# Neighbourhood attention trunk: a run's loads in one sequence, headed by a wait for a third of the transposes

## The chip, the cores and the metric

One core of a Trainium2 chip runs the whole kernel as one program. The metric is device time in microseconds; three runs of the kernel before gave 991.87, 992.1 and 993.92, so its median is 992.1. The profile is of one execution, on the hardware, with every instruction recorded.

## The reference

One layer of an encoder over 2048 tokens of 1024 columns, in float32. The tokens are a grid of 32 rows by 64 columns.

```python
h = rmsnorm(x, g)
q, k, v, gate = split(h @ w_in, 4)              # w_in: 1024 x 4096; 16 heads of 64
s = q . k / 8 + rel_pos_bias                    # each token sees 8 rows x 16 columns of the grid
o = softmax(s) @ v
x = x + (o * silu(gate)) @ w_out                # w_out: 1024 x 1024
out = rmsnorm(x, norm_f)
```

## The kernel before

All matrices are split into a high and a low part, so that a product of two takes three matmuls; large products are made from seven half-size products instead of eight. The order of every engine's instructions is written out by the program itself, in Python; nothing is rescheduled afterwards.

The program has three parts. In the first (to about 560 us) `stage_one` and `stage_two` form most of the queries, keys, values and gates and store them in HBM (`qd`, `kd`, `vd`, `sgd`). The second is the attention, 32 *runs* (lists `order`, `cycles = 32`): a run is a pair of heads `p` with a quarter `T` of the tokens. The third (`rows_by_seven`, from about 870 us) forms the output product and the last normalisation.

The main loop (L1825) has one body for each run. Body m does, in this order:

- `begin(m)` (L1804) puts the loads of the body on a list of things that fall due;
- `feed(...)` gives TensorE *fill*: some 14 matmuls per run of the remaining projections (L384 to L388) or, later, of the output product (L1600 to L1604). Each matmul of the fill advances a counted clock by one, and `due` (L336) issues whatever on the list has come due by that clock. The clock is counted while the program is written; nothing of it is read on the chip;
- `turns(m-1)` (L1358): 48 transposes on TensorE (L1372, tiles `ph`) turn the probabilities of run m-1, in three thirds `b`; after each third ScalarE and VectorE copy the two `ph` banks to the tile `PT` (named `pta`; L1378, L1376). Behind them GpSimd clears parts of the probability tiles (L1308, `clear_x`);
- `scores(2m)` and `scores(2m+1)` (L1310): 64 matmuls `s` of queries and keys (L1323), then on VectorE the sum with the bias table (L1332) and on ScalarE the exponential (L1340);
- `values(m-1)` (L1382): 36 matmuls `o` of `pta` and the values (L1395), then the product with the gates (L1399) and, 4 counts later, the store to `ogd` (L1402).

What a run reads from HBM is loaded by SyncE, in order, one DMA after the other:

- queries, `load_q` (L1243, tile `q`, 256 KB, two buffers);
- keys, `load_k` (L1226, tile `kt`, 128 to 512 KB; one buffer for even and one for odd `p`, and a run of the same `p` adds to it);
- two bias tables, `load_bias` (L1268, tile `em`, 184 or 253 KB each, ten buffers);
- values, `load_v` (L1252, tile `vt`, 480 KB, two buffers);
- gates, `load_sg` (L1260, tile `sgt`, 256 KB, two buffers).

Before, `begin(m)` asks for the gates of run m-1, the tables, queries and keys of run m+1 and the values of run m, in this order, one every half count from 0.5 on. On the chip SyncE issues a DMA when the ones ahead of it are issued, when the tile's last reader is done, and when the DMA eight places before it has landed, because eight completion semaphores are used in turn. A load thus goes out as soon as its buffer is free: the queries wait for the last scores matmul of the run that had the buffer (L1248), the values for its last `o` matmul (L1258).

In the same queue stand the weights of the fill (`raw`, L161 and L163), the stores, and from the last runs on the weights and rows of the third part: `land_first` (L1628) loads nine weights `t` at 1.5 counts of the last run's body, and six loads of attention output (`raw<-ogd`, L1656) follow from 10 counts on.

Of the kernel before, what the change touches and what calls it, by code (L numbers as in the profile page):

```python
# [61 lines left out]
def build(ctx, tc, x, xr, xt, wg, bias, w_out, n0, nf, out):  # L62
    nc = tc.nc
# [56 lines left out]
    def bank(n, name):  # L120
        return banks.tile([128, n], F32, name=name, tag="bank")
# [208 lines left out]
    def store(key, lag, f):  # L330
        n = len(later)
        while n and later[n - 1][0] > clock[0] + lag:
            n -= 1
        later.insert(n, (clock[0] + lag, key, f))
# [8 lines left out]
    def must(*keys):  # L343
        assert all(k in written for k in keys), keys
        for n in range(len(later) - 1, -1, -1):
            if later[n][1] in keys:
                for _ in range(n + 1):
                    later.pop(0)[2]()
                break
# [869 lines left out]
    KT, VT, QT, EM, SG = {}, {}, {}, {}, {}  # L1219
    stored_at = {}  # L1220
    order = [(p, T) for p in range(NP) for T in (1, 0)] + [(p, T) for p in range(NP - 2) for T in (2, 3)]
# [4 lines left out]
    def load_k(p, T):  # L1226
        r0, r1, more = PARTS[T]
        base = 12 * (T > 1)
        a, b = r0 * GW, r1 * GW + more
        must(*[("k", p, c) for c in range(a // 512, (b + 511) // 512)])  # L1230

        def keys():
            if T in (1, 2):
                khalf.clear()
                KT[p, T // 2] = (kp([128, 2048], F32, "kt") if p % 2 == 0 else mkp([128, 1536], F32, "kt"))[:, :1344]
            t = KT[p, T // 2]
            if T == 2:
                nc.gpsimd.memset(t[:, 1280:1288], 0.0)
            nc.sync.dma_start(t[:, a - base * GW:b - base * GW], kd[p][:, a:b])

        return keys

    def load_q(p, T):  # L1243
        must(("q", p, T))

        def queries():
            QT[p, T] = qp([128, 512], F32, "q")
            nc.sync.dma_start(QT[p, T], qd[p][T])  # L1248

        return queries  # L1250

    def load_v(p, T):  # L1252
        r0, r1 = FRAME[T], FRAME[T] + TALL
        must(*[("v", p // 4, t) for t in range(r0 // 2, (r1 + 1) // 2)])
        rows = vd[p // 4][p % 4][r0 * 8192:r1 * 8192].rearrange("(k x) -> k x", x=1024)
        t = vp([128, 1024], F32, "vt")
        VT[p, T] = t.rearrange("p (s d) -> p s d", s=8)
        nc.sync.dma_start(t[:8 * TALL], rows)  # L1258

    def load_sg(p, T):  # L1260
        must(("g", p, T))
        SG[p, T] = sp([128, 512], F32, "sgt")
        nc.sync.dma_start(SG[p, T], sgd[p][T])
# [4 lines left out]
    def load_bias(p, T):  # L1268
        fs = []
        kind = BRINGS[T]  # L1270
        w = 2 * WIDE * TABLES[kind][2]
        EM[p, T // 2, kind] = []
        for quad in range(2):
            t = mp([128, 512], F32, "em")[:, :w]
            EM[p, T // 2, kind].append([t[:, :w // 2], t[:, w // 2:]])
            o = TABLE_AT[kind] + quad * w
            fs.append(lambda t=t, o=o, w=w: nc.sync.dma_start(t, bias[p, 128 * o:128 * (o + w)].rearrange("(q c) -> q c", c=w)))
        return fs

    X, PT, ST = {}, {}, {}  # L1280
# [18 lines left out]
    def clear_x(T):  # L1299
        stale = []  # L1300
        for half in range(2):
            (u0, n0), (u1, n1) = held[half], HALF_ROWS[T][half]
            held[half] = u1, n1
            stale += [(half, a, b - a) for a, b in ((u0, min(u0 + n0, u1)), (max(u0, u1 + n1), u0 + n0)) if a < b]
        for quad in range(2):
            for half, a, n in stale:
                for s in range(2):
                    nc.gpsimd.memset(by_strip(X[quad, half, s], (a, n)), 0.0)  # L1308
# [49 lines left out]
    def turns(m):  # L1358
        p, T = order[m]
        k = 8 * TALL  # L1360
        PT[m] = pt([128, 3072], F32, "pta")
        t = PT[m].rearrange("p (s b n c) -> p b s n c", s=2, b=3, c=64)
        for b in range(3):
            ph = [bank(512, f"ph{h}") for h in range(2)]
            at = (2 - b) * k
            for quad in range(2):
                for half in range(2):
                    for s in range(2):
                        for h in range(2):
                            q = slice(64 * h, 64 * h + 64)  # L1370
                            o = s * 256 + half * 128 + quad * 64
                            nc.tensor.transpose(ph[h][:k, o:o + 64], X[quad, half, s][q, at:at + k], ident[q, q])  # L1372
            for h in range(2):
                o, i_ = t[:k, b, :, h::2], ph[h][:k].rearrange("p (s n c) -> p s n c", s=2, c=64)
                if h:
                    nc.vector.tensor_copy(o, i_)  # L1376
                else:
                    nc.scalar.activation(o, i_, AF.Copy)  # L1378
        if m + 1 < cycles:
            clear_x(order[m + 1][1])  # L1380

# [170 lines left out]
    def rows_due():  # L1552
        n = ready["split"]
        return (n < ready["loaded"] and "turn" in ready and place[n] <= ready["turn"] + 3 and now() - late["loaded_at"][n] >= 40 \
                and sum(1 if hasattr(g, "rearrange") else 2 for g in G.values()) <= 6)
# [95 lines left out]
    def load_rows_of(m, f, home=None):  # L1651
        n, half = PAIRS[m][int(f[1]) - 1], int(f[2]) - 1
        T, i = divmod(n, 4)
        must(*[("og", p, T) for p in range(NP) if p // 4 == half])
        A[m, f] = (home or raw)([128, 512], F32, "raw")
        nc.sync.dma_start(A[m, f].rearrange("p (k q) -> p k q", k=4), ogd[T][i, half])  # L1656
# [108 lines left out]
    cycles = len(order)  # L1765
# [30 lines left out]
    def later_loads(fs, lag, step):  # L1796
        for k, f in enumerate(fs):
            store(("load",), lag + k * step, f)

    def all_loads():  # L1800
        while any(e[1][0] == "load" for e in later):
            later.pop(0)[2]()

    def begin(m):  # L1804
        all_loads()
        quiet[0] = False
        fs = [lambda: load_sg(*order[m - 1])] if m else []
        if m + 1 < cycles:
            nx = order[m + 1]
            fs += load_bias(*nx)  # L1810
            fs += [load_q(*nx), load_k(*nx)]
        if m < cycles:
            fs.append(lambda: load_v(*order[m]))
        later_loads(fs, 0.5, 0.5)
        if m == cycles - 1:
            later_loads([land_first], 1.5, 0)
            later_loads([lambda f=f, i=i: load_rows_of(i, f) for i in ((2, 0, 1) if PLAIN <= 6 else (0, 1)) for f in ("A11", "A12")], 10, 0.5)
        if m == cycles:
            later_loads([land_rest], 4, 0)
# [5 lines left out]
    for m in range(cycles + 1):  # L1825
        a = amount[m] - 8
        begin(m)
        feed(HALF_HEAD)
        if m:
            normalise(2 * m - 1, 0)  # L1830
        feed(HEAD - HALF_HEAD)
        if m:
# [5 lines left out]
            most, behind = 99 if a > 12 else 0 if rows_due() else 1, bool(rooted)  # L1838
# [19 lines left out]
        if m:  # L1858
            turns(m - 1)
# [58 lines left out]
```

## Time and profile before

| | |
|---|---|
| runs of the kernel, us | 991.87, 992.1, 993.92 |
| profiled execution, us | 993.25 |
| its span, us | 991.5 |
| instructions | 22624 |
| granted TensorE clock | 0.999 of full speed |
| HBM read and written | 160.37 MB and 66.06 MB |
| attention runs | about 574 to 871 us, some 9.3 us each |

How to read it: PE is TensorE's matmuls, PEld its weight loads, DVE VectorE, ACT ScalarE, POOL GpSimd, SP SyncE; "SPq" is a DMA issue in SyncE's queue. L and a number is the line of the program. `ph<-ident,x` is an instruction that writes tile `ph` and reads `ident` and `x`. In the table of waits stand, for an engine and a line, whom it waited for, the total in us, how often, and the longest. "issue" there and in the chain is time in which an engine waited for nothing that the profile shows. A row of a stretch table has the stretch, its length, and busy time and count for PE, PEld, DVE, ACT and POOL, then the granted clock, the DMA engines' mean share and GB/s. A row of the DMA list has the issue, its count, its size, and the median time from issue to landing. A row of a DMA queue has its packets, their MB and the share of the 16 DMA engines.

### The profile page before, as it was taken

What the parts mean: (1) busy time and instruction counts of PE and PEld (TensorE: products, weight loads), DVE (VectorE), ACT (ScalarE), POOL (GpSimd) and SP (SyncE); (2) the same over time, 40 slices, a digit from 0 to 9 for tenths busy, and PEclk for the clock granted to TensorE, in tenths of its full rate; (3) what the DMA queues carried; (4) which work ended last, traced back from release to release, by engine and by line L of the source; (5) the groups of instructions that cost most, each with busy time, mean ns of one, the idle gap of its engine ahead of it and who ended that gap; (6) DMA issues with size and microseconds to landing.
All of it is one profiled execution on the core that took longest, in us unless ns stands there. A gap on an engine that the chain in (4) does not pass through costs nothing.

```text
span 991.5 us, 22624 instructions
## 1 busy us (share of the span) xinstructions
PE 979.3 (99%) x8172; PEld 797.0 (80%) x8172; DVE 755.2 (76%) x1735; ACT 531.5 (54%) x1310; POOL 159.6 (16%) x430
## 2 busy tenths in 40 slices
PE   9999999999999999999999999999999999999997
PEld 7888888888888888888888778777778777888886
DVE  6899888988665876766775677668778878877866
ACT  7773245455535342343433467677777776654443
POOL 0000001231100000000001133333343332302110
PEclk9999999999999999999999999999999999999999
DMA  8943547777957836657565799878989978697754
GB/s 287 337 130 102 196 132 256 248 242 251 368 159 225 276 116 201 189 182 224 169 176 203 247 302 271 264 226 279 307 277 288 298 222 266 223 379 212 205 146 117
DMA packets 149968, 227.93 MB, mean 230 GB/s; under 512 B 13536, under 2 KB 66016, under 8 KB 149856
## 3 DMA queue, kind: packets, MB, share of 16 engines
q1 hardware_dynamic: 146832, 221.37, 70.2%
q0 software_dynamic: 2592, 4.72, 2.8%
q8 instruction: 64, 1.05, 0.4%
q14 instruction: 48, 0.39, 0.1%
q10 hardware_dynamic: 432, 0.40, 0.1%
HBM read 160.37 MB, written 66.06 MB: 228 GB/s over the span
## 4 chain that ended last, share of the span: by engine, by line
PE 99%; issue 1%; DVE 0%; ACT 0%
PE pp L446 40%; PE pv L612 13%; PE py L1695 12%; PE o L1395 8%; PE s L1323 6%; PE ph L1372 5%; PE pp L388 2%; PE pp L384 2%; PE pp L386 2%; PE pv L727 2%; PE po L1600 2%; PE po L1604 2%; PE po L1602 2%; PE zp L127 0%; PE prb L235 0%
## 5 line engine op out<-in xcount | busy, mean ns | idle before, releaser
L446 PE MATMUL pp<-h,f 128*128 128x512 f32 x576 | 185.3, 389 | 0.0
L446 PE MATMUL pp<-t,f 128*128 128x512 f32 x702 | 171.4, 389 | 0.0
L446 PEld LDWEIGHTS pp<-t,f 128*128 128x128 f32 x702 | 131.8, 188 | 27.4
L1340 ACT ACTIVATE x<-sums,st 128x264 f32<-128x264 f32 (+1 forms) x256 | 124.5, 488 | 30.0 <-DVE st L1332 30.0
L446 PEld LDWEIGHTS pp<-h,f 128*128 128x128 f32 x576 | 108.1, 188 | 22.6
L446 PE MATMUL pp<-l,f 128*128 128x512 f32 x288 | 112.0, 389 | 0.0
L1352 POOL TENSOR_SCALAR x<-x,st 128x264 f32<-128x264 f32 (+1 forms) x192 | 88.5, 477 | 113.7 <-DVE st L1347 93.8
L1332 DVE CUSTOM_DVE_ANT_0 sums<-s,em 128x253 f32<-128x253 f32 (+1 forms) x256 | 91.1, 401 | 6.2 <-ACT x L1340 1.7
L429 DVE TENSOR_TENSOR f<-raw,f 128x512 fp32r<-128x512 f32 x105 | 75.9, 727 | 19.4 <-ACT f L428 19.3
L1395 PE MATMUL o<-pta,vt 120*64 120x192 f32 (+2 forms) x1152 | 85.1, 300 | 4.0 <-issue 4.0
L1395 PEld LDWEIGHTS o<-pta,vt 120*64 120x64 f32 x1152 | 70.2, 137 | 23.2 <-issue 16.4
L428 ACT ACTIVATE f<-raw 128x512 fp32r<-128x512 f32 x105 | 63.4, 622 | 36.6 <-DVE raw L435 22.0
L1376 DVE COPY pta<-ph 120x512 f32<-120x512 f32 x96 | 60.3, 684 | 18.3 <-PE ph L1372 18.1
L1378 ACT ACTIVATE pta<-ph 120x512 f32<-120x512 f32 x96 | 50.4, 599 | 37.8 <-PE ph L1372 37.8
L446 PEld LDWEIGHTS pp<-l,f 128*128 128x128 f32 x288 | 54.0, 188 | 11.3
L1323 PE MATMUL s<-kt,q 64*32 64x253 f32 (+1 forms) x2048 | 59.2, 362 | 0.7 <-issue 0.7
L1372 PEld LDWEIGHTS ph<-ident,x 64*120 64x120 f32 x1536 | 47.6, 135 | 11.3 <-issue 10.6
L612 PE MATMUL pv<-wh,t 128*128 128x512 f32 x176 | 56.2, 389 | 0.0
L1695 PE MATMUL py<-woh,f 128*128 128x512 f32 x168 | 55.4, 390 | 0.0
L467 POOL TENSOR_TENSOR tmp<-tmp,rb 128x512 f32<-128x512 f32 x18 | 28.5, 1582 | 157.6 <-DVE tmp L464 137.2
L446 PE MATMUL pp<-sixths,f 128*128 128x512 f32 x198 | 52.7, 389 | 0.0
L1372 PE MATMUL ph<-ident,x 64*120 64x64 f32 x1536 | 52.0, 221 | 0.0
(231 smaller groups left out, 1889.4 us busy)
## 6 DMA issues: line engine op xcount, KB each, us to landing
raw<-in_wg_dram SPq DMA_DIRECT2D x124, 256.0 KB, 4.8
vt<-vd SPq DMA_DIRECT2D x32, 480.0 KB, 5.2
row<-in_xr_dram SPq DMA_DIRECT2D x32, 256.0 KB, 5.2
vd<-v SPq DMA_DIRECT2D x32, 256.0 KB, 3.2
sgd<-sg SPq DMA_DIRECT2D x32, 256.0 KB, 3.8
q<-qd SPq DMA_DIRECT2D x32, 256.0 KB, 3.6
sgt<-sgd SPq DMA_DIRECT2D x32, 256.0 KB, 5.3
ogd<-og SPq DMA_DIRECT2D x32, 256.0 KB, 5.3
```

Of the source, the lines that this page charges most:

```text
L428: nc.scalar.activation(t[:, 0], src, AF.Copy)
L429: nc.vector.tensor_tensor(t[:, 1], src, t[:, 0].bitcast(F32), OP.subtract)
L446: nc.tensor.matmul(B[n, P], t[:, int(m == 2), c], x[k][int(m == 1)], start=P in (1, 6, 5) and k == 0 and m == 0, stop=k == 3 and m == 2, s ...
L612: nc.tensor.matmul(p, a[:, o], b, start=P in (1, 6, 5) and k == 0 and m == 0, stop=k == 3 and m == 2, skip_group_check=True)
L1323: nc.tensor.matmul(places[half, s][h * 32:h * 32 + 32], qt[a, g * 64 + half * 32:g * 64 + half * 32 + 32], kt[a, o:o + n * GW].rearrange(" ...
L1332: nc.vector.tensor_tensor_reduce(rows[s][:, :, :WIDE], places[half, s].rearrange("p (r c) -> p r c", c=WIDE), table[s].rearrange("p (r c) ...
L1340: nc.scalar.activation(to, rows[s].rearrange("p r (b c) -> p b r c", b=3), AF.Exp, bias=st[:, o:o + 1], scale=-1.0, accum_out=st[:, 4 + o: ...
L1352: nc.gpsimd.tensor_scalar(t, t, f, 1.0, op0=OP.mult, op1=OP.mult)
L1372: nc.tensor.transpose(ph[h][:k, o:o + 64], X[quad, half, s][q, at:at + k], ident[q, q])
L1376: nc.vector.tensor_copy(o, i_)
L1395: nc.tensor.matmul(o[s * 64:s * 64 + 64, g0 * 64:g1 * 64], vt[:k, strip, s * 64:s * 64 + 64], moving, start=strip == 0, stop=strip == 7, s ...
L1695: nc.tensor.matmul(B[m, P], t[:, a, c], b, start=P in (1, 6, 5) and k == 0 and i == 0, stop=k == 3 and i == 2, skip_group_check=True)
```

## The change

`load_q` takes an argument. Where it is given a part of a tile, GpSimd first copies its eight elements into the new query tile, and the DMA of the queries, which overwrites the tile, therefore waits for that copy. The new function `loads_of(m)` issues without any lag the queries, keys and tables of run m+1, then the values and gates of run m (the last run's gates excepted). It is called once in `begin(0)` for run 0, and from then on inside `turns(m)`, after the first third (`b == 0`), for run m+1, with the first eight elements of `PT[m]`, which ScalarE's first copy of that third has written. `begin` keeps the last run's gates, and the loads of the third part. Nothing that is computed changes.

```diff
     def load_q(p, T):
         must(("q", p, T))
 
-        def queries():
+        def queries(behind=None):
             QT[p, T] = qp([128, 512], F32, "q")
+            if behind is not None:
+                nc.gpsimd.tensor_copy(QT[p, T][:1, :8], behind)
             nc.sync.dma_start(QT[p, T], qd[p][T])
...
+            if b == 0 and m + 1 < cycles:
+                loads_of(m + 1, PT[m][:1, :8])
         if m + 1 < cycles:
             clear_x(order[m + 1][1])
...
+    def loads_of(m, behind=None):
+        if m + 1 < cycles:
+            nx = order[m + 1]
+            load_q(*nx)(behind)
+            load_k(*nx)()
+            for f in load_bias(*nx):
+                f()
+        load_v(*order[m])
+        if m < cycles - 1:
+            load_sg(*order[m])
+
     def begin(m):
         all_loads()
         quiet[0] = False
-        fs = [lambda: load_sg(*order[m - 1])] if m else []
-        if m + 1 < cycles:
-            nx = order[m + 1]
-            fs += load_bias(*nx)
-            fs += [load_q(*nx), load_k(*nx)]
-        if m < cycles:
-            fs.append(lambda: load_v(*order[m]))
-        later_loads(fs, 0.5, 0.5)
+        if m == 0:
+            loads_of(0)
+        if m == cycles:
+            load_sg(*order[m - 1])
```

SyncE's queue where the change shows, in a run near the end; names as above, `ogd` the store of a run's output, `xr` rows of the input. Before:

```order
L1248 DMA q<-qd_66 128x512
L1239 DMA kt<-kd_74 128x1024
L1258 DMA vt<-vd_84 120x1024
L1402 DMA ogd_87<-og 128x4x128
L1263 DMA sgt<-sgd_81 128x512
L1277 DMA em<-in_bias_dram 128x368 x2
```

The same place now:

```order
L1406 DMA ogd_87<-og 128x4x128
L1250 DMA q<-qd_66 128x512
L1239 DMA kt<-kd_74 128x1024
L1279 DMA em<-in_bias_dram 128x506 x2
L1260 DMA vt<-vd_84 120x1024
L1265 DMA sgt<-sgd_81 128x512
```

The tables and the gates have moved to the two sides of the values, and the store stands outside the sequence.

GpSimd's queue at the first such place (the probabilities `x` are scaled by `st`, then parts of them cleared). Before:

```order
L1352 TENSOR_SCALAR x_5195<-x_5195,st 128x3x88
L1352 TENSOR_SCALAR x_5197<-x_5197,st 128x3x88
L1308 MEMSET x_5191 128x3x24
L1308 MEMSET x_5193 128x3x24
L1308 MEMSET x_5201 128x3x32
```

The same place now:

```order
L1354 TENSOR_SCALAR x_5195<-x_5195,st 128x3x88
L1354 TENSOR_SCALAR x_5197<-x_5197,st 128x3x88
L1249 COPY q<-pta 1x8
L1310 MEMSET x_5191 128x3x24
L1310 MEMSET x_5193 128x3x24
```

The copy stands between the scaling and the clearing, 30 times in all.

## The prediction

> **What bounds the kernel now.** The page's first part comes first, then PE's own waits.
>
> ```profile
> PE 979.3 (99%) x8172; PEld 797.0 (80%) x8172; DVE 755.2 (76%) x1735; ACT 531.5 (54%) x1310; POOL 159.6 (16%) x430
> ```
>
> The table of what PE waited for (total us, times, longest):
>
> ```profile
> PE o L1395 <- issue: 4.0, 4, 2.1
> ...
> PE s L1323 <- issue: 0.7, 1, 0.7
> ```
>
> TensorE is the bound from end to end. No semaphore holds it after the start: no load, table or value is ever late for it. What it loses inside the program is 4.0 + 0.7 = 4.7 us, in five gaps called "issue", that is, with nothing to wait for in the profile. All five lie in the attention runs. The chain around one of them, and the groups between one gap's end and the next's (us, then busy time and count by engine):
>
> ```profile
> 781.19 1.56 PE ph L1372 x48
> ...
> 784.38 2.55 PE o L1395 x36
> ...
> 790.33 1.56 PE ph L1372 x48
> 791.89 1.87 PE s L1323 x64
> 793.75 0.58 PE o L1395 x6
> 794.34 0.74 issue
> ```
>
> ```profile
> 590.60:626.60 36.00, 35.65 (x631) 28.14 (x632) 26.73 (x97) 24.60 (x76) 11.82 (x44) 1.00 0.91 272
> 626.60:663.41 36.81, 36.07 (x631) 28.50 (x631) 26.01 (x101) 25.91 (x84) 13.71 (x48) 1.00 0.84 260
> 663.41:729.29 65.88, 65.00 (x1135) 51.44 (x1136) 50.77 (x188) 50.09 (x158) 24.49 (x88) 1.00 0.86 262
> 729.29:795.07 65.78, 65.04 (x1136) 51.73 (x1136) 54.29 (x193) 50.70 (x160) 23.95 (x85) 1.00 0.93 295
> ```
>
> Matmuls and weight loads together: 1263, 1262, 2271, 2272, which is 5, 5, 9 and 9 times 252.5. So the gaps sit on a grid of PE's instructions. The queue table and two stretches of the DMA list say whose grid:
>
> ```profile
> q8 instruction: 64, 1.05, 0.4%
> ```
>
> ```profile
> q1 hardware_dynamic: 1149, 1.53, 95.6%
> q14 instruction: 1, 0.01, 0.4%
> ```
>
> ```profile
> q1 hardware_dynamic: 136, 0.23, 41.7%
> q8 instruction: 1, 0.02, 4.1%
> ```
>
> Queue 8 brings 64 packets of 16 KB, and 16344 matmuls and weight loads over 64 are 255: one packet is one block of PE's program. The second fence is 787.0 to 792.5 us, with no packet of queue 8; the third is 792.5 to 794.0, with one; PE stands from 794.34. PE ran out of instructions because the next block came late. Counted back from the gap, 253 instructions are 12 (o), 128 (s), 96 (ph) and 17 of the fill before them, whose 28 or so take the 3.4 us from 786.93 to 790.33: the block then running began near 790.33 - 2.0 = 788.3, and I take it that the next is asked for there. It moved only after 792.5, over 4 us later. What SP had issued by then:
>
> ```profile
> 784.51 0.33 SPq L1248 DMA_DIRECT2D q<-qd  x1
> 784.88 0.43 SPq L1239 DMA_DIRECT2D kt<-kd  x1
> 786.97 0.34 SPq L1258 DMA_DIRECT2D vt<-vd  x1
> 787.70 0.38 SPq L1402 DMA_DIRECT2D ogd<-og  x1
> 788.13 0.49 SPq L1263 DMA_DIRECT2D sgt<-sgd  x1
> 788.67 0.97 SPq L1277 DMA_DIRECT2D em<-in_bias_dram  x2
> ```
>
> The values (480 KB) go out as the products of a run end, with a store and the gates straight behind, just when such a block is asked for. The packet behaves as if it stood behind them: 1.0 MB in 4.2 us is 240 GB/s.
>
> **The change part by part.** PE, DVE and ACT keep their order row for row; only SP's queue and 30 small POOL copies differ. SP in a late run before (q queries, kt keys, em tables, vt values, sgt gates, ogd the store of a run's output):
>
> ```order
> L1263 DMA sgt<-sgd_81 128x512
> L1277 DMA em<-in_bias_dram 128x368 x2
> L1248 DMA q<-qd_66 128x512
> L1239 DMA kt<-kd_74 128x256
> L1258 DMA vt<-vd_84 120x1024
> L1402 DMA ogd_88<-og 128x4x128
> ```
>
> and now:
>
> ```order
> L1250 DMA q<-qd_66 128x512
> L1239 DMA kt<-kd_74 128x256
> L1279 DMA em<-in_bias_dram 128x368 x2
> L1260 DMA vt<-vd_84 120x1024
> L1265 DMA sgt<-sgd_82 128x512
> L1406 DMA ogd_87<-og 128x4x128
> ```
>
> One sequence, headed by the queries; gates and values are now those of one and the same run, and the store stands behind all.
>
> (1) *The 30 copies.* SP's and POOL's waits, and the prices of their parts:
>
> ```profile
> SPq L1248 <- PE s L1323: 66.9, 25, 5.4
> SPq L1258 <- PE o L1395: 46.9, 29, 7.2
> ```
>
> ```profile
> POOL x L1308 <- PE ph L1372: 75.8, 30, 3.5
> ```
>
> ```profile
> 799.19 0.10 POOL L1238 MEMSET kt<- 128x8 f32 x1
> ```
>
> ```profile
> 781.84 1.58 ACT L1378 ACTIVATE pta<-ph 120x512 f32<-120x512 f32 x3 [0.51 <-PE ph L1372]
> ```
>
> A copy of eight elements is priced as the memset of eight, 0.10 us: 30 x 0.10 = 3 us of a POOL that is busy for 16%. Behind it on POOL stand the clearing memsets of L1308, which already wait for the same transposes. On the path: 0.
>
> (2) *When the loads go.* The first ACT eviction ends at 781.84 + 1.58/3 = 782.4, 1.2 us after the transposes began at 781.19. With the copy and two hand-overs the queries go out some 1.5 to 1.7 us after the first transpose, the other five within 2.5 us more (0.33 to 0.49 each above). Both engine waits of SP go: queries no longer follow the last scores, values no longer the last product. Landing, in us from issue:
>
> ```profile
> vt<-vd SPq DMA_DIRECT2D x32, 480.0 KB, 5.2
> ...
> q<-qd SPq DMA_DIRECT2D x32, 256.0 KB, 3.6
> sgt<-sgd SPq DMA_DIRECT2D x32, 256.0 KB, 5.3
> ...
> em<-in_bias_dram SPq DMA_DIRECT2D x32, 253.0 KB, 5.7
> ...
> kt<-kd SPq DMA_DIRECT2D x8, 484.0 KB, 6.0
> ```
>
> The second table, issued near +2.9, lands near +8.6; the next scores begin at +9.14 + 1.56 = +10.7. Values land near +8.7 and are wanted at +9.1 + 3.4 = +12.5. Margins of 2 and 4 us; cost 0. If that cover fails by 0.25 us in each of 30 runs, it costs 7.5.
>
> (3) *The block fetches.* A block asked for at 788.3 is +7.1 in its run. The new sequence is all issued by +4.2, its last load landing near +9, that is 790.2; only the store may stand behind. So the packet starts some 2 us earlier than it did, and the gap was 0.74. The largest gap, 2.1, has the same shape in a crowded run. Blocks asked for between +2 and +5 meet the sequence itself: there the delay grows to 4 us or so, against a block that lasts 253 of the run's 324 or so instructions, 7 us. I take 0.4 us for what remains, between 0 and half of today's 4.7. [...]
>
> (4) *The last run's values.* They are now asked for behind the weights of the end. SP before, and now:
>
> ```order
> L1263 DMA sgt<-sgd_82 128x512
> L1258 DMA vt<-vd_84 120x1024
> L1624 DMA t<-wodT_95 128x512 x8
> L1624 DMA t<-wodT_96 128x512
> L1402 DMA ogd_87<-og 128x4x128
> L1520 DMA out_dram<-y 128x512 x2
> L1656 DMA raw<-ogd_87 128x512 x2
> L1656 DMA raw<-ogd_86 128x512 x4
> ```
>
> ```order
> L1628 DMA t<-wodT_95 128x512 x8
> L1628 DMA t<-wodT_96 128x512
> L1406 DMA ogd_87<-og 128x4x128
> L1524 DMA out_dram<-y 128x512 x2
> L1660 DMA raw<-ogd_87 128x512 x2
> L1660 DMA raw<-ogd_86 128x512 x4
> L1260 DMA vt<-vd_84 120x1024
> ```
>
> The load has moved past 18 others. Their times, and when PE wants the values:
>
> ```profile
> 852.10 0.34 SPq L1258 DMA_DIRECT2D vt<-vd  x1
> 852.53 5.55 SPq L1624 DMA_DIRECT2D t<-wodT  x9
> ...
> 860.85 6.52 SPq L1656 DMA_DIRECT2D raw<-ogd  x6
> 867.47 0.38 SPq L1263 DMA_DIRECT2D sgt<-sgd  x1
> ```
>
> ```profile
> 846.32 1.56 PE ph L1372 x48
> ...
> 868.19 2.55 PE o L1395 x36
> ```
>
> If nothing before it moved, the values would go out at 867.47 and land 5.2 later at 872.7: PE stands for 4.5 us. But the weights no longer wait behind a values load: they can start at 846.32 + 4.2 = 850.5, 2.0 us sooner, and 480 KB less stand in front, 2.0 us at the 240 GB/s above, less where the queue moves faster. Issue near 864, landing near 869.2: 1.0 us of stall, between 0 and 4.5, nearer the low end because SP in this stretch is held by landings, which all move.
>
> *The sum.* The profiled execution took 993.25 us, a span of 991.5 and 1.75 around it, 1.15 above the median of 992.1; executions differ in just such gaps, so I build on the part without them: 993.25 - 4.7 = 988.5. Then 988.5 + 0.4 + 1.0 = **989.9 us**.
>
> **The rivals.** A measurement here tells some 0.2%, 2.0 us, from no change: faster means below 990.1, slower above 994.1.
>
> *The gaps stay.* Six loads of 1.6 MB in a row are a denser burst than now, and other blocks are caught in it; or the fetch has a latency of its own. For it: the bytes are the same, the DMA share between gaps is 0.84 to 0.93 already. Against: the five gaps all follow a values load at the end of the products. At today's typical 992.1 - 988.5 = 3.6 of gaps plus 1.0 at the end: 993.1. [...]
>
> *The last values are late by the full 4.5.* With the gaps gone: 988.5 + 0.4 + 4.5 = 993.4, no change to be seen.
>
> *The wait does nothing,* because SP comes to the queries after the copy anyway: 992.1. Against: SP stands at L1248 in 25 of the runs, from before the last scores end.
>
> *Slower: tables late in every run.* Nothing is asked for before +1.5. If SP's issues take the 1 us and more that a full queue gives them, instead of 0.4, the second table lands after +10.7 and scores or DVE wait. It decides from 2 us of added delay; 0.25 us a run are 989.9 + 7.5 = 997.4.
>
> **How the numbers follow.** My case, gaps mostly gone and the end nearly covered: 0.52. Gaps stay 0.26, last values late 0.09, wait without effect 0.03: these land within 0.2%, 0.38. Tables late: 0.10. The range leaves the last out: from 988.4, no gap and no stall, to 993.0, where the gaps stay.
>
> **What would show it.** Right: PE's "issue" total below 1.5 us; SP's waits on L1323 and L1395 gone and one on POOL in 30 runs; a new PE wait at the last o of about 1 us on the values' DMA. Wrong: "issue" of 3 us or more; PE or DVE waiting for q, kt or em in the runs; a wait above 3 us at the last o.

## The result, and the profile after

The changed kernel took 1003.43 us in the median of four runs (1002.54 to 1006.46), the kernel before, beside it, 991.99 (990.95 to 993.92): a ratio of 1.0118, 95% interval 1.0092 to 1.0145. It is slower by 11.4 us, above the range of 988.4 to 993.0 and above the dearest of the rivals, 997.4. The profiled execution took 1003.03 us, with a span of 1001.1 and a granted clock of 0.995 (before: 993.25, 991.5, 0.999).

TensorE's waits in the changed kernel (total us, times, longest):

```profile
PE o L1399 <- DMA vt<-vd: 9.3, 5, 4.6
...
PE o L1399 <- ACT x L1342: 0.9, 1, 0.9
PE o L1399 <- issue: 0.6, 2, 0.4
```

The gaps called issue went from 4.7 to 0.6 us, as forecast. But values are late five times, for 9.3 us, where nothing was late before. To see where, both programs are cut at the same matmuls of TensorE; ahead of the attention and in the last 470 matmuls they agree to 0.2 us, and between these lie 500 matmuls with the first runs, 4500 with the middle, and 300 with the last run. Stretch and length, TensorE's busy time and count, granted clock, DMA share, GB/s; before:

```profile
547.82:594.82 47.00, 44.94 (x501) 1.00 0.88 273
594.82:851.99 257.17, 254.47 (x4507) 1.00 0.86 265
851.99:878.07 26.08, 26.08 (x303) 1.00 0.92 311
```

and after:

```profile
547.96:597.03 49.07, 46.49 (x501) 0.97 0.78 233
597.03:855.40 258.37, 254.69 (x4507) 1.00 0.91 266
855.40:887.70 32.30, 27.65 (x303) 0.95 0.99 342
```

In this pair of executions the stretch of the last run costs 6.2 us, that of the first runs 2.1, the long middle 1.2. In the first runs and in the last one TensorE is also *busy* for longer (46.49 against 44.94, 27.65 against 26.08), at a clock of 0.97 and 0.95. The chain there shows why. First place, then last place:

```profile
581.91 7.29 DMA vt<-vd
...
589.33 4.23 PE o L1399 x36
```

```profile
869.92 6.19 DMA vt<-vd
...
876.24 4.14 PE o L1399 x36
```

The 36 products after a late landing take 4.23 and 4.14 us; undisturbed they took 2.55. The clock just behind the two waits, and during the second (stretch; busy time and count of PE, PEld, DVE, ACT, POOL; clock; DMA share; GB/s):

```profile
589.30:592.00 2.70, 2.67 (x22) 2.45 (x24) 0.00 (x0) 1.31 (x6) 0.96 (x3) 0.50 1.06 384
...
871.60:876.20 4.60, 0.00 (x0) 0.00 (x0) 2.58 (x4) 3.37 (x8) 0.00 (x0) 0.98 0.96 274
876.20:878.00 1.80, 1.76 (x17) 1.68 (x19) 0.00 (x0) 0.00 (x0) 0.00 (x0) 0.50 1.09 398
```

TensorE stands for 2.6 and 4.6 us, and then runs at half its clock for 3.4 us (589.26 to 592.68 and 875.98 to 879.40 by the trace's clock records): each of the two waits is paid a second time, by 1.6 to 1.7 us. My sum had no such term.

How late the loads are, from the page's DMA issues (median us from issue to landing; before: values 5.2, queries 3.6, gates 5.3):

```profile
vt<-vd SPq DMA_DIRECT2D x32, 480.0 KB, 7.0
...
q<-qd SPq DMA_DIRECT2D x32, 256.0 KB, 3.9
sgt<-sgd SPq DMA_DIRECT2D x32, 256.0 KB, 7.1
```

The head of the sequence lands as it did; what stands fifth and sixth in it takes 1.8 us longer.

### The profile page after: what moved, and what is told of

It reads as the page before. It is cut to its first block, busy times and chain, and to the rows that moved or that the text cites. A ratio compares the mean times of both kernels' runs of the same rounds, so it can differ in the third digit from the quotient of the medians.

```text
span 1001.1 us, 22693 instructions
## 1 busy us (share of the span) xinstructions
PE 982.8 (98%) x8172; PEld 800.9 (80%) x8172; DVE 754.7 (75%) x1735; ACT 532.0 (53%) x1310; POOL 162.4 (16%) x460
## 4 chain that ended last, share of the span: by engine, by line
PE 94%; DMA 4%; SPq 1%; issue 0%; ACT 0%; DVE 0%; POOL 0%; ACTq 0%
PE pp L446 40%; PE pv L612 13%; PE py L1699 11%; PE o L1399 8%; PE s L1325 5%; PE ph L1374 4%; DMA vt<-vd 3%; PE pv L727 2%; PE pp L388 2%; PE pp L384 2%; PE pp L386 2%; PE po L1604 1%; PE po L1608 1%; PE po L1606 1%; DMA sgt<-sgd 1%; SPq L1239 0%
## 5 line engine op out<-in xcount | busy, mean ns | idle before, releaser
L1399 PE MATMUL o<-pta,vt 120*64 120x192 f32 (+2 forms) x1152 | 87.9, 307 | 10.9 <-DMA vt<-vd 9.3
L1399 PEld LDWEIGHTS o<-pta,vt 120*64 120x64 f32 x1152 | 73.8, 141 | 29.8 <-issue 12.0
```

The lines of the kernel that those rows point to most:

```text
L1399: nc.tensor.matmul(o[s * 64:s * 64 + 64, g0 * 64:g1 * 64], vt[:k, strip, s * 64:s * 64 + 64], moving, start=strip == 0, stop=strip == 7, s ...
```

## The experiments

Theory A: the loss is values that come late at three places (first runs; near 738 to 760 us, where three 512 KB loads `ograw` of attention output stand in the queue; last run), each paid again by half clock. Theory B: holding the loads back for the transposes costs a little in every run. Theory C: the program is granted less clock as a whole. All medians, with the kernel before run beside on the same chip:

| kernel | us | before | ratio, 95% interval |
|---|---|---|---|
| last_v | 999.65 | 992.64 | 1.0072, 1.0047 to 1.0097 |
| no_wait | 1001.63 | 992.64 | 1.0100, 1.0062 to 1.0137 |
| v_head | 1000.54 | 992.64 | 1.0080, 1.0049 to 1.0112 |
| before_v_late | 995.68 | 992.64 | 1.0030, 1.0011 to 1.0048 |
| head_only (runs 0 to 2) | 993.57 | 992.16 | 1.0013, 0.9999 to 1.0028 |
| middle (3 to 26) | 995.63 | 992.16 | 1.0028, 1.0015 to 1.0042 |
| middle_cut (3 to 15, 21 to 26) | 996.03 | 992.16 | 1.0042, 1.0026 to 1.0058 |
| tail_only (27 to 31) | 999.68 | 992.16 | 1.0063, 1.0039 to 1.0088 |
| tail_v9 | 992.86 | 991.98 | 1.0013, 1.0000 to 1.0026 |
| mid_early (3 to 15) | 994.76 | 991.98 | 1.0034, 1.0016 to 1.0051 |
| mid_late (21 to 26) | 992.41 | 991.98 | 0.9998, 0.9986 to 1.0009 |
| mid_3_8 | 992.63 | 992.19 | 1.0003, 0.9989 to 1.0018 |
| mid_9_15 | 992.05 | 992.19 | 1.0002, 0.9990 to 1.0015 |
| mid_nowait (3 to 15) | 994.41 | 992.19 | 1.0032, 1.0012 to 1.0052 |
| mid_qke (3 to 15) | 995.60 | 992.19 | 1.0030, 1.0015 to 1.0044 |
| after_v9 | 996.96 | 992.56 | 1.0046, 1.0027 to 1.0065 |
| after_v9_h | 995.51 | 992.56 | 1.0028, 1.0014 to 1.0042 |

**Parts of the change, undone or done alone.** `last_v`: the changed kernel, with the last run's values asked for at the start of its body, ahead of the weights of the end.

```
     def loads_of(m, behind=None):
...
-        load_v(*order[m])
         if m < cycles - 1:
+            load_v(*order[m])
             load_sg(*order[m])
...
         if m == cycles - 1:
+            load_v(*order[m])
             later_loads([land_first], 1.5, 0)
```

> The changed kernel, with one load put elsewhere: the last run's values are asked for at the start of the last run's body, ahead of the nine weights of the end, instead of behind them. Theory A (late values at three places: near 587, near 738 to 760 and at the last product; each wait is paid a second time because TensorE's clock is granted at 0.50 for about 2.5 us after a wait of that length): the last place goes, its wait of 4.6 us and about 1.6 us of half clock, so some 6 us less than the changed kernel, 997 us; the waits at the other two places stay as they are. Theory B (holding every load back until the transposes is what costs, spread over the runs): the time stays within 2 us of the changed kernel's 1003.4. Theory C (this program is granted less clock, whatever it waits for): stays at 1003.

It gave 999.65: a third of the loss back, not the 6 us of theory A. Its waits, and its queue in the last run:

```profile
PE py L1699 <- ACT f L1665: 2.8, 1, 2.8
```

```profile
851.35 0.47 SPq L1260 DMA_DIRECT2D vt<-vd  x1
...
853.16 0.34 SPq L1260 DMA_DIRECT2D vt<-vd  x1
853.55 8.47 SPq L1628 DMA_DIRECT2D t<-wodT  x9
```

The wait has moved: now the rows of the output product, which ScalarE forms (`f`) from the six loads of attention output, are 2.8 us late. Two values loads stand back to back ahead of the weights, and the nine weights take 8.47 us to issue; before, they took 5.55. So it was not the last values alone; the queue of the end is late as a whole.

`no_wait`: the changed kernel without the 30 copies.

```
-                loads_of(m + 1, PT[m][:1, :8])
+                loads_of(m + 1)
```

> The changed kernel without the 30 copies: the same one sequence of loads at the same place in the program, but each load goes out as soon as SP reaches it and its buffer is free. Theory A: the last values stay behind the weights, so the wait at the end stays (about 4 us and its half clock); near 587 and near 740 the loads go out some 2 us sooner and the waits there shrink to 1 us or less: 997 to 999 us. Theory B: all of the loss comes back, 992 us. If the gaps called issue come from loads standing in front of a block of instructions, they come back in part here, 1 to 4 us; in the changed kernel they are 0.6 us.

1001.63. The wait for the transposes is not the cost: theory B, as I had put it, falls. `v_head`: values and gates ahead of queries, keys and tables, the copy put on the values.

```
     def loads_of(m, behind=None):
+        load_v(*order[m], behind)
+        if m < cycles - 1:
+            load_sg(*order[m])
         if m + 1 < cycles:
             nx = order[m + 1]
-            load_q(*nx)(behind)
+            load_q(*nx)()
...
-        load_v(*order[m])
-        if m < cycles - 1:
-            load_sg(*order[m])
```

> The changed kernel with the sequence turned round: values and gates first (the copy now heads the values), then queries, keys and tables. The last run's values stay behind the weights. Theory A: the values land about 2 us sooner in each run, so the waits on them near 587 and 738 to 760 go or shrink below 1 us (2 to 5 us less, half clock included), the wait at the end stays: 998 to 1001 us. A risk that A names: the tables now come last and may be late where the queue is full near 740. Theory B: no change, 1003.

1000.54, and the waits of its profile:

```profile
PE o L1401 <- DMA vt<-vd: 4.5, 1, 4.5
PE s L1327 <- DMA kt<-kd: 3.4, 1, 3.4
```

The 4.5 us at the end stay. In the first runs it is now the keys, moved behind values and gates, that come late, near 585 us.

`before_v_late`: the kernel before, with only the last run's values moved behind the end's loads.

```
-        if m < cycles:
+        if m < cycles - 1:
             fs.append(lambda: load_v(*order[m]))
...
+            later_loads([lambda: load_v(*order[m])], 13, 0)
```

> The kernel before with that one load alone moved: the last run's values are asked for behind the nine weights, the store, the two outputs and the six loads of attention output, where the change puts them. Theory A: a wait of 4 to 5 us at the last product and about 1.6 us of half clock behind it: 992 + 6 = 998 us, all of it at the end of the runs; the issue gaps stay at 3 to 5 us. Theory B: 992 to 993 us.

995.68, where theory A had 998, with one wait for those values:

```profile
PE o L1395 <- DMA vt<-vd: 2.4, 1, 2.4
```

That place alone costs 3 us, in a queue that is otherwise the old one; in the new queue the end costs more than twice that.

**Which runs.** In the next kernels the bodies whose number is in a set load as in the changed kernel, all others as before.

```
+    IN_ONE = set(range(27, 32))
...
-            if b == 0 and m + 1 < cycles:
+            if b == 0 and m + 1 in IN_ONE:
                 loads_of(m + 1, PT[m][:1, :8])
...
+        if m not in IN_ONE:
+            if m + 1 < cycles:
+                nx = order[m + 1]
+                fs += load_bias(*nx)
+                fs += [load_q(*nx), load_k(*nx)]
+            if m < cycles:
+                fs.append(lambda: load_v(*order[m]))
```

> The kernel before with the new sequence in the bodies of runs 0 to 2 alone. Theory A: one wait for values of about 2.5 us near 587 us, then 36 products in 4.2 instead of 2.55 us; the gap of 2.1 us that the kernel before has there goes: 994, plus or minus 1. Theory B: three runs by 0.34, 993.

> The new sequence only in the bodies of runs 3 to 26; the first three and the last five load as before. Theory A (the loss is three places at which values come late, each followed by products at half clock): the first and the last place go; the place near 738 to 760 us, where three 512 KB loads of attention output stand in the queue, stays with about 2.7 us of waits for values; four of the gaps called issue shrink, 3.5 us of gain; together within 1 us of before, about 992. Theory B (a burst of six loads costs a little in every run, 11 us over 32 runs, 0.34 each): 24 runs, about 1000.

> As the kernel with the sequence in runs 3 to 26, but runs 16 to 20, where the loads of attention output stand, load as before too. Theory A: no wait for values anywhere; the gaps called issue go except in the bodies that load as before: 2 to 3 us below before, 989 to 990. Theory B: 19 runs by 0.34 us, about 998. If both fall: no difference from before, though the gaps are gone, would say that a fetch gap costs the program nothing in the median.

> The kernel before with the new sequence in the bodies of runs 27 to 31 alone. Theory A: the wait for the last run's values, 4.5 us, and 1.6 us of half clock behind it: 998. Theory B: five runs by 0.34, 993.7.

Measured over before: 1.4 (its interval still touches no change), 3.5, 3.9 and 7.5 us. First, middle and last together are 12.4; the whole change costs 11.4. So it adds up, and two thirds lie in the last five runs. Theory A is right there: in tail_only's profile the last products stood for 4.2 us, and half clock followed. (The table of waits names ScalarE there, but the values went out at 861.90, flew 6.3 us, and TensorE went on at 868.32.) In the first runs it is not shown clear of noise: the profile of head_only, its quickest execution, has 1.4 us at the matmul where the changed kernel waited 2.56, again until values landed (out at 581.15, 6.9 us of flight), and no half clock behind it. In the middle it is wrong: leaving out the five runs beside `ograw` (middle_cut) gives nothing back, though its profile has almost no wait for values left:

```profile
PE o L1399 <- issue: 4.3, 5, 2.1
...
PE s L1325 <- issue: 0.7, 1, 0.7
PE pp L388 <- issue: 0.4, 1, 0.4
PE o L1399 <- DMA vt<-vd: 0.2, 1, 0.2
```

Theory B's price of 0.34 us a run is too high everywhere. Theory C falls, since the clock is low only behind the long waits.

**The tail's mechanism.** SyncE in the last run of the changed kernel:

```profile
851.30 0.32 SPq L1250 DMA_DIRECT2D q<-qd  x1
851.68 0.68 SPq L1239 DMA_DIRECT2D kt<-kd  x1
852.41 0.90 SPq L1279 DMA_DIRECT2D em<-in_bias_dram  x2
853.40 0.38 SPq L1260 DMA_DIRECT2D vt<-vd  x1
853.83 0.39 SPq L1265 DMA_DIRECT2D sgt<-sgd  x1
854.32 7.36 SPq L1628 DMA_DIRECT2D t<-wodT  x9
862.01 0.37 SPq L1406 DMA_DIRECT2D ogd<-og  x1
...
863.86 5.96 SPq L1660 DMA_DIRECT2D raw<-ogd  x6
869.92 0.37 SPq L1260 DMA_DIRECT2D vt<-vd  x1
```

The weights follow straight behind the six loads of the run before, and take 7.36 us to issue where they took 5.55; the store of the output goes out behind them, and the values last of all. `tail_v9` is tail_only with one row moved: the last values go out behind the store, ahead of the two outputs and the six loads `raw`.

```
-        load_v(*order[m])
         if m < cycles - 1:
+            load_v(*order[m])
             load_sg(*order[m])
...
             later_loads([land_first], 1.5, 0)
+            later_loads([lambda: load_v(*order[m])], 9.5, 0)
```

> As the kernel with the sequence in runs 27 to 31 alone, except that the last run's values are asked for 9.5 counts into the body, right behind the store of a run's output and ahead of the two outputs and six loads of attention output. Theory A (the tail's loss is the queue: the values stand behind loads that themselves wait for that store to land): values out some 12.7 us after the transposes of the run before the last began, landed near 18.5, wanted at 21.9: no wait, no half clock, 992 to 993. Rival (the bytes decide: two values loads and the weights in one burst make whatever stands last late): the rows of the output product come 2 to 3 us late, 996 to 997.

992.86. The row of the last run's 300 matmuls, in tail_only and then in tail_v9:

```profile
847.91:879.92 32.01, 27.81 (x302) 0.95 1.00 350
```

```profile
856.44:882.52 26.08, 26.08 (x302) 1.00 1.03 354
```

The same bytes in the same five runs, 32.01 and 26.08 us: the place in the queue decides, not the bytes. In the whole changed kernel, `after_v9` moves that one row, and `after_v9_h` lets the first three runs load as before too:

> The changed kernel with a single row of SyncE's queue moved: the last run's values go out behind the store of a run's output instead of behind the two outputs and six loads of attention output that follow it. If the place of that load is the tail's whole loss (992.9 with it, 999.7 without it, in the last five runs alone): 6 to 7 us below the changed kernel, 996 to 997, with no wait for values at the end. If the burst decides in the whole kernel: about 1000, with the rows of the output product late.

> As that, with the first three runs loading as before too. If the first place costs what the runs 0 to 2 alone showed, 1.4 us: 995 to 995.5. What is then left above the 992 of before is the part of runs 3 to 26, which has no place yet: about 3 us.

996.96 and 995.51, both as expected. Each taken over the kernel before beside it, the change costs 11.4 us, 4.4 with that row moved and 2.9 with the first runs left alone too: one row of the queue is worth 7.0 us, the first runs 1.5 (less than these intervals can tell from nothing), and 2.9 are left for runs 3 to 26. No version here beats the kernel before.

**The fetch of TensorE's instructions.** `fetch_alone` drops the kernel and measures the mechanism of step 3 by itself.

```
+    for form in ("none", "one", "burst", "spread"):
+        for _ in range(16):
+            for i in range(5):
+                if form == "spread":
+                    read(k, i)
+                    load(k, i)
+                elif i == 0:
+                    for n in range(5):
+                        read(k, n)
+                    for n in range(5 if form == "burst" else 1 if form == "one" else 0):
+                        load(k, n)
+                work(60)
+            k += 1
```

> Nothing of the reference is computed: TensorE alone does 4 times 16 turns of 300 transposes (like those of L1372 in the kernel before, some 10 us a turn) that wait for nothing; SyncE loads beside it, per turn: nothing; one load of 512 KB; five loads of 1.75 MB in a burst at the turn's start; the same five spread over the turn. Theory F (TensorE's instructions come in blocks of 16 KB through a DMA queue and wait behind loads that are under way): no gap called issue beside no loads, gaps of tenths of a microsecond up to 2 us beside the burst, fewer beside the spread loads. [...]

Its four stretches of 4800 transposes (length; busy time and count of PE, PEld, DVE, POOL; clock; DMA share; GB/s), its waits and its instruction queue:

```profile
3.90:147.90 144.00, 144.00 (x4800) 144.00 (x4802) 0.00 (x0) 0.00 (x0) 1.00 0.03 10
147.90:296.40 148.50, 143.39 (x4807) 142.31 (x4803) 0.00 (x0) 0.00 (x0) 1.00 0.18 54
296.40:464.40 168.00, 150.38 (x4811) 147.81 (x4808) 0.00 (x0) 0.00 (x0) 0.98 0.55 176
464.40:620.50 156.10, 148.48 (x4807) 145.35 (x4804) 0.00 (x0) 0.00 (x0) 1.00 0.61 187
```

```profile
PE ph L96 <- issue: 30.3, 37, 2.1
```

```profile
q8 instruction: 151, 2.47, 1.5%
```

Length less busy time is 0, 5.1, 17.6 and 7.6 us. Without loads TensorE never stands. With one load of 512 KB a turn it does, with five in a burst more than three times as much, and the same five spread over the turn cost less than half of that. (Busy time rises by the reads of the loaded tiles, 0.05 to 0.06 us each, and by half clock behind the longest gaps: the 3.73 us behind the one of 2.11 us had a clock of 0.57.) Every gap over 60 ns begins at the same place of a grid of 128 matmuls with their 128 weight loads; the 38442 matmuls and weight loads of the four stretches over the 151 packets of queue 8, 16 KB each, are 255. These packets show the wait itself. Where nothing is loaded, such a packet starts in the median 0.3 us after a block's first matmul; with one load 1.1 us after it, with bursts 1.7 us (at most 3.8), with the same loads spread 1.6 us (at most 2.6). Behind every gap TensorE goes on 1.2 to 1.6 us after the packet's end. So it does in the kernel before: behind all of its five gaps, 1.3 to 1.4 us after the end of a packet. That is theory F. How much of the loads goes ahead of such a packet, no run here shows.

**What the middle costs.** Six kernels split runs 3 to 26.

> The new sequence only in the bodies of runs 3 to 15. Spread cost (3.3 us over 24 runs by the kernel with runs 3 to 26, 0.14 each): 994, that is 1.8 above before. A cost at one place in the later runs: no difference from before, 992.

> The new sequence only in the bodies of runs 21 to 26. Spread cost: 0.8 us, 993. A cost at one place in these runs: 995 or more.

> The new sequence only in the bodies of runs 3 to 8. If the 2.8 us of runs 3 to 15 are spread over them: 993.3, 1.3 above before. If they come from the first of them, where the queue still holds the weights of the projections: 994 to 995; if from the later ones: 992, as before.

> The new sequence only in the bodies of runs 9 to 15. Spread: 993.5. From the later ones of runs 3 to 15: 994 to 995; from the first ones: 992.

mid_nowait is mid_early without the copies (the edit of no_wait); mid_qke leaves values and gates of runs 3 to 15 as before:

```
     def loads_of(m, behind=None):
...
-        load_v(*order[m])
-        if m < cycles - 1:
-            load_sg(*order[m])
...
+        if m < cycles:
+            fs.append(lambda: load_v(*order[m]))
         later_loads(fs, 0.5, 0.5)
```

> The new sequence in the bodies of runs 3 to 15, without the copies that hold the queries back. If holding the loads back is what costs there: 992 to 993. If it is the burst, or the order: 994.8, as with the copies.

> In the bodies of runs 3 to 15 only the queries, keys and tables go out in one sequence behind the copy; values and gates load as before. If the six loads in one burst cost the time (block fetches that wait behind them, as the kernel with TensorE alone showed: 17.6 us of gaps beside bursts, 7.6 beside the same bytes spread): 992 to 993. If the late queries, keys and tables do: 994.8.

Runs 21 to 26 cost nothing. Runs 3 to 15 cost 2.8 us, whether the loads wait or not (2.2) and whether the values and gates are in the burst or not (3.4). But runs 3 to 8 alone and 9 to 15 alone show 0.4 and nothing; the upper ends of their intervals, 0.18% and 0.15%, together come to 0.33%, just short of the 0.34% of the whole, whose own interval begins at 0.16%. No trace names a place. The kernel with runs 3 to 26 was profiled near its median (995.71 us), and cut at the same matmuls its 4500 of the middle took 257.37 us, the kernel before's 257.17; what it took longer lay ahead of the attention (1.7 us) and in the last 470 matmuls (1.0), where its loads stand as before. One reason is that executions differ by as much: the 4500 matmuls of the middle in tail_only and in tail_v9, in which nearly all those runs load as before, and in mid_qke:

```profile
594.39:847.91 253.52, 253.33 (x4506) 1.00 0.85 267
```

```profile
598.63:856.44 257.81, 254.51 (x4506) 1.00 0.84 259
```

```profile
595.06:855.76 260.70, 256.24 (x4506) 0.99 0.86 266
```

Two executions of nearly the same instructions (the quickest of tail_only's and the slowest of tail_v9's) are 4.3 us apart, so a difference of 3 us can't be found by laying one profile beside another. What the 3 us of runs 3 to 26 are stays open.

## Why the prediction was wrong

Between the forecast of 989.9 and the 1003.4 measured lie 13.5 us. By the runs above some 6 are the last values (7.0 instead of 1.0), some 3 a gain in the gaps that the median does not show (3.6 of gaps cut to 0.4), 1.5 the first runs, and 2.9 runs 3 to 26, both put at nothing.

**Step 4, the last run's values, failed by its size.** It had 1.0 us; the wait was 4.65, and half clock behind it made 6.2: the sign of being wrong, a wait above 3 us at the last products, came. It put the issue near 864 and the flight at 5.2. The transposes of the run before began at 849.72 instead of 846.32, so 864 is 867.4 in this profile. They went out at 869.92, 2.5 later, and flew 6.19, 1.0 longer: 1.0 + 2.5 + 1.0 = 4.5. The weights did start about where I had put them (853.9 by the working, 854.32). What I left out stood right ahead of them: the queries, keys, tables, values and gates of the run before. Before, those had gone out ahead of the transposes, the gates last, at 844.34:

```profile
840.72 0.33 SPq L1248 DMA_DIRECT2D q<-qd  x1
```

Now it is from 851.30 on, 1.6 us behind their start. I counted what the weights no longer wait for, and not what the same change puts in its place; so the weights took 7.36 us to issue (for 1.9 us of it SyncE waited until the values and gates of that sequence had landed) and the store, 4 us sooner by the working (858.97 before, so near 858.4 here), came at 862.01. The price of "between 0 and 4.5" was bounded by landings as they were before, and half clock lay outside of it.

**Step 2, the loads of each run at no cost, failed at one of its two margins.** The queries went out 1.6 us after the first transpose, as forecast (849.72 to 851.30); SyncE's long waits on scores and products were gone and it waited for GpSimd in 30 runs, as forecast too; and no table was late in the profile. But the values' margin of 4 us came from a flight of 5.2 us and an issue at +3.5. In the first runs the queue holds more than the sequence:

```profile
577.16 3.75 SPq L1239 DMA_DIRECT2D kt<-kd  x1
...
581.91 0.44 SPq L1260 DMA_DIRECT2D vt<-vd  x1
```

The keys took 3.75 us to issue, behind weights and a row of the input; so the values went out 7.2 us after the first transpose (574.71) instead of 3.5, flew 7.29 us and came 2.56 late. My rival "tables late in every run" had named just this, an issue of more than 1 us in a full queue, but priced it for the tables and for all runs alike; it struck the values, in single runs. That rival's time, 997.4, was nearest of all, for another reason than the one it gave.

**Step 3, the block fetches, was right in its mechanism and wrong in its weight.** The fetch behind loads is shown by fetch_alone, and the gaps of the changed kernel's profile fell to 0.6 us. But the 4.7 us were one execution's. In the five profiles of kernels that load runs 3 to 26 as before, these gaps were 1.4 (tail_only), 1.7 (head_only), 3.6 (before_v_late), 4.7 and 4.9 us (tail_v9); in the seven with the sequence in all of those runs, 0 (v_head) to 2.8 (after_v9); in the seven with it in a part of them, 1.4 (mid_nowait) to 6.0 (mid_qke). The means of the first two groups, 3.3 and 1.4, point to a gain of some 2 us, but the groups overlap, and I had no ground to count 4.3 us of gain in a median. They can also grow: in after_v9 one fetch was 2.3 us late, and half clock followed:

```profile
662.75 2.31 issue
...
665.68 4.22 PE o L1399 x36
```

**Step 1, the copies at nothing, held** as far as the runs tell: mid_nowait and mid_early are 0.35 us apart, no_wait and the changed kernel 1.8, both inside their intervals.

**The chances.** 0.10 for slower was too little. The rival with the last values late by the full 4.5 us, at 0.09, was right on that wait, and still put the time at 993.4. All of the cases took the loads' flights from the profile of before, and none asked what flights become when six loads go out within 2.5 us instead of over a whole run.

## What to carry to other kernels

When loads are moved later as a group, look at the two ends of the loop first: list what stands in the queue behind the group there, and give each of those its new time, not only the load that changed places. A wait of TensorE can cost more than its length, for the slow clock behind it: the two here of 2.56 and 4.65 us were paid again by 1.6 to 1.7 us, and the shortest that half clock followed was 1.67 us (tail_v9). The gaps that had no releaser and sat on a grid of matmuls and weight loads, 252.5 in the kernel before and 256 in fetch_alone, were late blocks of program: TensorE went on 1.2 to 1.6 us after the end of a packet of queue 8. The size of such a gap in one profile is that of one execution.

## What the runs showed of the hardware

Half clock followed some waits of TensorE and not others. In these traces gaps of 1.67 (tail_v9), 2.11 (fetch_alone), 2.31 (after_v9), 2.56 and 4.65 us (changed kernel) were followed by it, while one of 1.62 us (changed kernel, near 738 us), one of 2.06 us (before, near 589 us) and another of 2.1 us (after_v9, near 741 us, with its 36 products in 2.62 us) were not. The clock records explain most of this. Ahead of the last matmul a drop lasts 3.41 us (6.83 in v_head), and the full clock between two drops a whole number of such steps: 283.31 us, or 83, in the changed kernel, and 20.48 us, or 6, in fetch_alone. So the traces have a grid of steps, and the three gaps without a drop were each cut in two by its border (at most 0.99, 1.04 and 1.49 us in one step). Over all profiles TensorE's standing within one step was never followed by half clock up to 1.57 us, always from 2.11 us on, and sometimes between: 1.67, 1.70, 1.83 and 1.98 us were, 1.75, 1.78, 1.81 and 2.05 us were not. One of 1.67 us in one step was enough (tail_v9; length, busy time and count of PE, clock, DMA share, GB/s):

```profile
590.87:594.28 3.41, 1.74 (x15) 1.00 1.03 383
594.28:597.69 3.41, 3.41 (x9) 0.50 0.95 244
```

SyncE's issue of one DMA took from 0.32 us (queries, 851.30) to 3.75 us (keys, 577.16) in the changed kernel's profile, and the flight of the same 480 KB from 5.2 us in the median before to 7.0 after.
